# Sixteen units of the third FFN as seven block products instead of eight, in a two-layer attention/mLSTM network

## The chip, the cores and the metric

The kernel runs on one core of one Trainium2 chip. The time is device microseconds of that core, from the runs; beside it stands one profiled execution, whose span and instructions the quoted views show. In those views PE is the matrix engine (PEld its weight loads), DVE the vector engine, ACT the scalar engine, POOL is GpSimd, SP the engine that issues most transfers.

## What is computed

The reference is a network of two layers on 256 latent and 256 context tokens of width 1024. Each layer is a half FFN, a mixer (attention in the first layer, mLSTM in the second) and another half FFN, each with a modulation by `c` ahead of it and a residual with layer norm behind it. The third FFN, the first of layer 1, is the place of the change:

```
def half_ffn(h, shift, scale, gate, w_in, w_out, g, b):
    xm = modulate(h, shift, scale)
    a, u = jnp.split(xm @ w_in, 2, axis=-1)
    y = (jax.nn.silu(a) * u) @ w_out
    return post_norm(h, 0.5 * gate * y, g, b)
```

`w_in` is 1024 × 5632 (`a` and `u` have 2816 columns each), `w_out` 2816 × 1024, all in 32-bit floats.

## The kernel before

Activations lie transposed: 128 features on the partitions, 512 tokens along the row, first the latent ones (`LAT`, 256) and then the context ones (`CTX`, 256), in eight blocks of features (`ND`). Precision is kept by splitting every operand into a high part, rounded to the matrix engine's 32-bit format, and a low part, what is left. `mm3` (line 208) multiplies with three products: high × high (L211), high × low (L214), low × high (L215). `split` (line 193) makes the parts: ACT casts the high one (L194), DVE subtracts for the low one (L199).

Weights come in chunks of 128 × 1024, 512 KB. `raw` (line 173) loads one into one of `RAW` = 3 buffers by a transfer that SP issues (L179); `pair` gives one of `WB` = 7 buffers for a high and a low part; `chunk` does load and split. `Stream` splits a chunk when it is first asked for, `Keep` also holds the chunks for a second use.

`ffn` (line 525) works in 22 units of 128 hidden columns. `unit_in` makes one: for each of eight feature blocks k and the two parts `a` and `u` three products, 48 in all, of 512 columns, into two of the six PSUM buffers `mm`. `ffn_g` (line 500) then applies SiLU on ACT (L521), multiplies on DVE (L522) and splits the result. The units go in two parts of 11. After each part `unit_out` makes the outputs of eight blocks d, 33 products each, and DVE adds them with the gate to the residual `h` (L557); in the last part `add_sum` (L357) also begins the sum for the norm.

Two places work on half the columns. The first four units (`LEAD`) take `LAT` and then `CTX`, so that they can begin before the context tokens' norm is done. The last four blocks of the last part (`TAIL`) take all `LAT` outputs and then all `CTX` outputs, so that the next norm can begin. `TAILSTEP` says after which product which step of that norm is woven in: `b` begins it, `m` and `c` subtract the mean block by block, `v` makes the variance, `r` the scale, `x` the normalised blocks. `ENDSTEP` does the first steps for `CTX` behind the tail.

The modulation of later stages is made beside the FFN: `ada` (line 296) loads 512 KB of `ada_w` (L284, two buffers) and makes a dot product on DVE (L290). `pop` in `side` (line 1283) takes two from a queue after each unit and each output block of the first part; for the third FFN the queue has 32 of one dot each.

What decides the order: the instructions are traced in program order, and the framework orders each engine's queue ahead of time, earlier-traced ones first, but moves one forward whose inputs and buffers it expects ready. So chunks are loaded and split ahead of their use. An instruction that passes through `pin` (line 359) stays behind the one traced before it on its engine; the dots, the norm's products and its scale are pinned. On the chip every engine works through its queue in that fixed order.

Of the kernel before, what the change touches and what calls it, by code (L numbers as in the profile page):

```python
# [37 lines left out]
HEADS = 8  # L38
MH = 4
QK_SCALE = 128.0 ** -0.5  # L40
BIG = 1.0e30

RAW = 3
WB = 7
# [97 lines left out]
class Body:  # L142
# [137 lines left out]
    def ada_load(self, layer, dt):  # L280
        if (layer, dt // ND) not in self.mod:
            self.mod[layer, dt // ND] = self.t([P, 2, ND])
        r = self.t([P, 1024], tag="ada", bufs=2, pool=self.gp)
        self.nc.sync.dma_start(r, self.a["ada_w"][layer, dt])  # L284
        return r
# [239 lines left out]
    def ffn(self, layer, s, gate, groups, side, start=None):  # L525
        nc, V = self.nc, self.nc.vector
        li = layer * 2 + s
        allg = BOTH
        call = lambda *k: side.get(k, lambda: None)()
        with self.tc.tile_pool(name=f"ffn{li}", bufs=1) as gp:  # L530
            self.gp, self.gt, self.gw, self.gn = gp, {}, T, NFH
            done = 0
# [12 lines left out]

            def unit_out(hf, d, w, g, steps={}):
                t0, t1 = g
                y = self.mm()
                for i in range(NFH):
                    gh, gl = self.gt[hf * NFH + i]  # L550
                    self.mm3(y[:, : t1 - t0], w(d * NFH + i), (gh[:, t0:t1], gl[:, t0:t1]), i == 0, i == NFH - 1)
                    self.steps(steps.get((int(g == CTX), d - (ND - TAIL), i), ""))
                for gg in groups:
                    if gg[0] >= t0 and gg[1] <= t1:
                        v = 0 if gg[0] == 0 else 1
                        z = self.h[:, d, gg[0] : gg[1]]
                        V.scalar_tensor_tensor(z, y[:, gg[0] - t0 : gg[1] - t0], gate()[:, v, d : d + 1], z, ALU.mult, ALU.add)  # L557
                        if hf:
# [4 lines left out]
            for hf in range(2):  # L563
                js = list(range(hf * NFH, (hf + 1) * NFH))[0 if hf else done :]
# [17 lines left out]
                if not hf:  # L582
                    self.residual(len(self.later))
                w = Stream(self, [w_out[hf * NFH + i] for i in range(NFH)])
                body = ND - TAIL if hf else ND
                for d in range(body):
                    unit_out(hf, d, w, allg)
                    call("out", hf, d)
                if body < ND:
                    w = Keep(self, w.chunks, SH, w)  # L590
                    self.fine = True
                    for g in groups:
                        for d in range(body, ND):
                            unit_out(hf, d, w, g, TAILSTEP)
                    self.steps(ENDSTEP)


    def ffn_last(self, layer, gate):
# [663 lines left out]
def emit(ctx, tc, a, out):  # L1262
# [19 lines left out]

    def side(key, coef, keep=(True, True), nxt=True, ada=(), alone=False):
        def pop():
            for _ in range(3 if len(ada) > 40 else 2):
                if ada:
# [4 lines left out]
        b.begin = lambda g: b.norm(g, get, keep[0 if g == LAT else 1], nxt, alone)  # L1291
        s = {}
        for j in range(NF):
            s["in", j] = pop
# [12 lines left out]
    assert not queue[1]  # L1307
    b.ffn(1, 0, once("g2", lambda: b.half_gate(1, 2)), both, side("n3", lambda: b.ln_mod(1, 0, (1, 3)), (True, False), ada=queue[2]))
    assert not queue[2]
# [8 lines left out]
def _layout(inputs):  # L1318
# [9 lines left out]
    w = f("ffn_w_in").reshape(4, ND, P, 2, NF, P).transpose(0, 4, 2, 1, 3, 5)  # L1328
    w_in = w.reshape(4, NF, P, 2, 1024).transpose(0, 1, 3, 2, 4).reshape(4, 2 * NF, P, 1024).copy()
    A["ffn_in"] = w_in  # L1330
    A["start_in"] = w[0, :NSTART].transpose(2, 1, 0, 3, 4).reshape(ND, P, 1024)
    w = f("ffn_w_out").reshape(4, 2, NFH, P, ND, P).transpose(0, 1, 4, 2, 3, 5)
    A["ffn_out"] = w.reshape(4, 2 * NFH, 8, P, P).transpose(0, 1, 3, 2, 4).reshape(4, 2 * NFH, P, 1024)
    A["ffn_last"] = f("ffn_w_out")[1, 1].reshape(NF, P, D)
# [64 lines left out]
```

## Time and profile before

| what | us |
|---|---|
| median of 3 runs | 1701.09 |
| lowest and highest run | 1696.46 and 1701.3 |
| span of the profiled execution | 1693.6 |
| PE busy in it | 1643.8 |
| DVE busy | 1231.7 |
| ACT busy | 656.3 |

The span is the time from the first to the last instruction of one execution, so it lies a little under the times of the runs. Busy time is the time in which an engine had at least one instruction at work; engines work beside each other, so the rows don't add up. An engine's share of the whole span says little about one stage. The prediction therefore takes windows of the trace that hold one kind of work.

### The profile page before, as it was taken

The numbers are of one execution on the slowest core, as the hardware profiler recorded it, in microseconds if no ns is written. First come the engines' busy times: TensorE is split into PE (matmuls) and PEld (weight loads), VectorE is DVE, ScalarE is ACT, GpSimd is POOL, SyncE is SP. The second block draws the span as 40 slices with busy tenths as digits, with TensorE's granted clock in tenths as the row PEclk, the third lists the DMA queues.
The fourth block names the chain that finished last, engine by engine and source line by source line (L and its number), as shares of the span: only waits on it lengthen the run. The fifth ranks groups of instructions, "written<-read, shape, count | busy, mean of one in ns | idle before, by whom it ended". The sixth has DMA issues, their size and how long they took to land.

```text
span 1693.6 us, 24765 instructions
## 1 busy us (share of the span) xinstructions
PE 1643.8 (97%) x9432; PEld 1441.6 (85%) x9432; DVE 1231.7 (73%) x2681; ACT 656.3 (39%) x1125; POOL 93.6 (6%) x114
## 2 busy tenths in 40 slices
PE   7999999999899999999999999999999999999997
PEld 6888888899887898888888998888889878999986
DVE  6799977659988899996334977643335967998687
ACT  5622133215465452212331543213322645556541
POOL 0000000002321100000000100000001001120000
PEclk9999999999999999999999999999999999999999
DMA  9576765412102346774222257642221232337542
GB/s 356 184 230 231 236 210 199 149 62 77 61 2 82 119 136 234 229 244 152 93 94 75 101 179 247 215 144 98 99 100 63 94 125 76 113 125 246 178 168 94
DMA packets 71910, 250.49 MB, mean 148 GB/s; under 512 B 7920, under 2 KB 10480, under 8 KB 71792
## 3 DMA queue, kind: packets, MB, share of 16 engines
q1 hardware_dynamic: 71072, 248.15, 43.1%
q8 instruction: 74, 1.21, 0.3%
q10 hardware_dynamic: 720, 0.76, 0.1%
q14 instruction: 44, 0.36, 0.1%
HBM read 247.83 MB, written 1.05 MB: 147 GB/s over the span
## 4 chain that ended last, share of the span: by engine, by line
PE 83%; DVE 11%; ACT 3%; DMA 2%; issue 1%; POOL 0%; ACTq 0%; DVEq 0%; SPq 0%
PE t L214 23%; PE t L215 23%; PE t L211 23%; PE t L668 4%; DVE t L199 3%; PE t L1165 2%; PE t L726 2%; PE t L728 2%; PE t L727 2%; ACT t L194 1%; PE t L380 1%; DVE t L473 1%; DVE t L400 1%; DVE t L475 1%; DVE t L1201 1%
## 5 line engine op out<-in xcount | busy, mean ns | idle before, releaser
L211 PE MATMUL t<-t,t 128*128 128x512 f32 (+2 forms) x2540 | 856.1, 339 | 10.1 <-ACT t L194 7.5
L214 PE MATMUL t<-t,t 128*128 128x512 f32 (+2 forms) x2540 | 858.5, 339 | 1.8 <-DVE t L475 1.3
L215 PE MATMUL t<-t,t 128*128 128x512 f32 (+2 forms) x2540 | 854.4, 337 | 1.9 <-DVE t L199 1.9
L199 DVE TENSOR_TENSOR t<-t,t 128x256 fp32r<-128x256 f32 (+2 forms) x793 | 494.8, 659 | 196.4 <-ACT t L194 195.8
L194 ACT CAST t<-t 128x1024 fp32r<-128x1024 f32 (+2 forms) x463 | 397.7, 880 | 587.0 <-PE t L215 311.2
L211 PEld LDWEIGHTS t<-t,t 128*128 128x128 f32 x2540 | 476.6, 188 | 65.7 <-ACT t L194 9.8
L214 PEld LDWEIGHTS t<-t,t 128*128 128x128 f32 x2540 | 477.7, 188 | 56.5 <-DVE t L475 2.5
L215 PEld LDWEIGHTS t<-t,t 128*128 128x128 f32 x2540 | 477.5, 188 | 55.3 <-DVE t L199 2.8
L290 DVE SCALAR_TENSOR_TENSOR t<-t,t 128x1024 bf16<-128x1024 f32 x224 | 262.6, 1220 | 15.9 <-DMA t<-in_ada_w 15.4
L522 DVE TENSOR_TENSOR t<-t,t 128x512 f32<-128x512 f32 (+1 forms) x93 | 54.0, 585 | 112.1 <-PE t L215 92.4
L521 ACT ACTIVATE t<-t 128x512 f32<-128x512 f32 (+1 forms) x93 | 47.4, 515 | 196.9 <-PE t L215 195.0
L417 POOL TENSOR_TENSOR t<-t,t 128x256 f32<-128x256 f32 x30 | 23.3, 777 | 1161.4 <-ACT t L407 1159.9
L557 DVE SCALAR_TENSOR_TENSOR t<-t,t,t 128x256 f32<-128x256 f32 x96 | 42.7, 478 | 54.2 <-PE t L215 54.2
L726 PE MATMUL t<-t,t 128*128 128x256 f32 (+1 forms) x256 | 80.4, 316 | 0.0
L728 PE MATMUL t<-t,t 128*128 128x256 f32 (+1 forms) x256 | 79.7, 314 | 0.0
L727 PE MATMUL t<-t,t 128*128 128x256 f32 (+1 forms) x256 | 79.5, 313 | 0.0
L1165 PE MATMUL t<-t,t 128*128 128x512 f32 (+1 forms) x248 | 54.8, 373 | 11.0 <-ACT t L274 5.2
L1165 PEld LDWEIGHTS t<-t,t 128*128 128x128 f32 x248 | 46.4, 220 | 19.0 <-ACT t L274 5.2
L668 PE MATMUL t<-t,t 128*128 128x512 f32 x264 | 60.0, 389 | 0.0
L668 PEld LDWEIGHTS t<-t,t 128*128 128x128 f32 x264 | 49.5, 188 | 10.2
L407 ACT ACTIVATE t<-t 128x256 f32<-128x256 f32 x72 | 26.1, 413 | 68.3 <-DVE t L400 68.3
L726 PEld LDWEIGHTS t<-t,t 128*128 128x128 f32 x256 | 49.6, 194 | 3.1 <-DVE t L789 0.3
(164 smaller groups left out, 1067.6 us busy)
## 6 DMA issues: line engine op xcount, KB each, us to landing
t<-in_ffn_in SPq DMA_DIRECT2D x168, 512.0 KB, 4.0
t<-in_ada_w SPq DMA_DIRECT2D x139, 512.0 KB, 4.2
t<-in_ffn_out SPq DMA_DIRECT2D x66, 512.0 KB, 3.7
t<-in_ffn_last SPq DMA_DIRECT2D x22, 512.0 KB, 3.7
t<-in_att_in SPq DMA_DIRECT2D x12, 512.0 KB, 3.5
t<-in_att_out SPq DMA_DIRECT2D x8, 512.0 KB, 3.9
t<-in_ml_qk SPq DMA_DIRECT2D x8, 512.0 KB, 3.4
t<-in_ml_v SPq DMA_DIRECT2D x8, 512.0 KB, 4.0
```

Of the source, the lines that this page charges most:

```text
L194: self.behind(self.nc.scalar.copy(h, x))
L199: self.behind(self.nc.vector.tensor_tensor(out=ls, in0=xs, in1=hs.bitcast(F32), op=ALU.subtract))
L211: ins = mm(out, wh, xh, start=first, stop=False)
L214: mm(out, wh, xl, start=False, stop=False)
L215: mm(out, wl, xh, start=False, stop=last)
L290: ins = nc.vector.scalar_tensor_tensor(self.tmp().bitcast(BF16), r, 1.0, self.cb[:, v, :], ALU.mult, ALU.mult, accum_out=to)
L522: V.tensor_tensor(out=sl, in0=sl, in1=pu[:, :n], op=ALU.mult)
L668: pin(nc.tensor.matmul(ys[tt][i], gs[g], ws[k][w][:, i * 512 : (i + 1) * 512], start=k == 0 and g == w == 0, stop=k == NF - 1 and g == 1,))
L726: mm(o, self.xh[:, k, c], wh, start=k == 0, stop=False)
L727: mm(o, self.xh[:, k, c], wl, start=False, stop=False)
L728: mm(o, self.xl[:, k, c], wh, start=False, stop=k == ND - 1)
L1165: mm = lambda *k, **kw: pin(nc.tensor.matmul(*k, **kw))
```

## The change

In the third FFN the units are divided into parts of 6, 8 and 8 (`FOLD`). The first six are made as before. The other sixteen use a scheme of Strassen's kind (Winograd's form). The product of a unit is seen as a 2 × 2 block product: the weights' rows `a` and `u` against two halves of the 1024 features, and the features' halves against `LAT` and `CTX`. Eight block products become seven, each over four feature blocks and 256 columns with three products a block: 84 of 256 columns instead of 48 of 512.

- `fold_x` makes the four sums of the activations, in two calls during the outputs of the first part. Three go to new tiles, one takes the place of the `CTX` columns that nobody reads any more.
- `fold_w` makes, per unit, four sums of the weights in place in the two raw buffers, and splits the unit's first chunk, half of the second, and both buffers of sums. For the second buffer of sums DVE doesn't subtract: ACT writes the high part and its negative, and a transfer issued by GpSimd adds the raw sums to the negative.
- `folded` makes the seven products into three PSUM buffers, adding some products onto earlier ones, with copies by ACT and sums by DVE between. Two units are interleaved: the last two products of one unit stand among those of the next, and the last unit's among the first outputs.
- The layout of the weights in memory is rearranged to suit.
- The tail has six blocks (`FOLDTAIL`) with a step table of its own. `RAW` is 4 in the whole kernel, the modulation's loads have one buffer in this FFN instead of two, and the queue is emptied by `FOLDPOP`: 12 dots by the first part's units, 4, 8 and 8 by the outputs of the three parts, of which the last six are traced behind the tail. `RING` sets the space for descriptors of GpSimd's transfers to 1024 bytes.

```diff
+FOLD = {2: (6, 8, 8)}
+FOLDTAIL = 6
+FOLDPOP = ((2, 2, 2, 2, 2, 2), (4, 8, 8))
+RING = 1024
-RAW = 3
+RAW = 4
+FOLDSTEP = {(0, 5, 1): 'bmccccccc', (1, 0, 2): 'c', (1, 0, 6): 'v', (1, 2, 1): 'rxxxxxxxx'}
...
-        r = self.t([P, 1024], tag="ada", bufs=2, pool=self.gp)
+        r = self.t([P, 1024], tag="ada", bufs=self.nada, pool=self.gp)
...
+                folded = None
+                if fold and hf:
+                    folded = self.folded(js, w_in)
+                    js = []
...
-                w = Stream(self, [w_out[hf * NFH + i] for i in range(NFH)])
-                body = ND - TAIL if hf else ND
-                for d in range(body):
+                w = (Keep if fold else Stream)(self, [w_out[ends[hf] - parts[hf] + i] for i in range(parts[hf])])
+                body = ND - tail if last else ND
+                begun = 0
+                if folded:
+                    n, begun = parts[hf], 2
+                    ys = [self.mm() for _ in range(2)]
+                    part_out(hf, 0, w, allg, ys[0], range(4))
+                    next(folded)
+                    part_out(hf, 0, w, allg, ys[0], range(4, n - 1))
+                    next(folded, None)
+                    part_out(hf, 1, w, allg, ys[1], range(n - 1))
+                    for d in range(2):
+                        part_out(hf, d, w, allg, ys[d], (n - 1,))
+                        sum_out(hf, d, allg, ys[d])
+                        call("out", hf, d)
+                for d in range(begun, body):
                     unit_out(hf, d, w, allg)
                     call("out", hf, d)
+                    if fold and not hf and d in (1, 4):
+                        self.fold_x(d // 2)
...
-                            unit_out(hf, d, w, g, TAILSTEP)
+                            unit_out(hf, d, w, g, tailstep)
+                    for d in range(body, ND):
+                        call("out", hf, d)
                     self.steps(ENDSTEP)
...
+    def fold_x(self, k):
+        V, S = self.nc.vector, self.nc.scalar
+        if k == 0:
+            self.th, self.tl = (self.t([P, 3, ND // 2, TL], F32R, pool=self.gp) for _ in range(2))
+        def whole(d, g):
+            f = self.tmp().rearrange("p (d f) -> p d f", d=2)
+            h, l = (x[:, d : d + 2, g[0] : g[1]].bitcast(F32) for x in (self.xh, self.xl))
+            V.tensor_tensor(out=f, in0=h, in1=l, op=ALU.add)
+            return f
+        f11, f12, f21, f22 = whole(k, LAT), whole(k, CTX), whole(ND // 2 + k, LAT), whole(ND // 2 + k, CTX)
+        V.tensor_tensor(out=f11, in0=f11, in1=f12, op=ALU.subtract)
+        V.tensor_tensor(out=f12, in0=f22, in1=f12, op=ALU.subtract)
+        V.tensor_tensor(out=f22, in0=f22, in1=f11, op=ALU.add)
+        V.tensor_tensor(out=f21, in0=f22, in1=f21, op=ALU.subtract)
+        ks = slice(k, k + 2)
+        to = [[x[:, i, ks, :] for x in (self.th, self.tl)] for i in range(3)]
+        to3 = [x[:, ks, CTX[0] : CTX[1]] for x in (self.xh, self.xl)]
+        self.split(f11, *to[0])
+        h, l = to[1]
+        S.activation(h, f22, AF.Copy, scale=-1.0)
+        V.scalar_tensor_tensor(l, f22, -1.0, h.bitcast(F32), ALU.mult, ALU.subtract)
+        self.split(f12, *to3)
+        self.split(f21, *to[2])
...
+    def fold_w(self, j, w_in):
+        V = self.nc.vector
+        r0, r1 = (self.raw(w_in[2 * j + i]) for i in range(2))
+        a = slice(0, 512), slice(512, 1024)
+        ps = [self.pair(sh=SH)]
+        self.split(r0, *ps[0])
...
+        w22 = [x[:, c] for x in p]
+        self.split(r1[:, a[0]], *w22)
+        V.tensor_tensor(out=r1[:, a[0]], in0=r1[:, a[0]], in1=r1[:, a[1]], op=ALU.add)
+        V.tensor_tensor(out=r1[:, a[1]], in0=r1[:, a[1]], in1=r0[:, a[0]], op=ALU.add)
+        V.tensor_tensor(out=r0[:, a[0]], in0=r0[:, a[0]], in1=r1[:, a[0]], op=ALU.add)
+        V.tensor_tensor(out=r0[:, a[1]], in0=r0[:, a[1]], in1=r0[:, a[0]], op=ALU.add)
+        for r in (r0, r1):
+            p = self.pair(sh=SH)
+            if r is r1:
+                self.nc.scalar.copy(p[0], r)
+                self.nc.scalar.activation(p[1], r, AF.Copy, scale=-1.0)
+                self.nc.gpsimd.dma_start(p[1], r, accum_op=ALU.add)
+            else:
+                self.split(r, *p)
+            ps.append(p)
...
+        def begin(j):
+            w = self.fold_w(j, w_in)
+            o0, o1, o2 = (self.mm()[:, :TL] for _ in range(3))
+            sl, u = self.tmp(), self.tmp()
+            product(o0, w["11"], "b11", True)
+            S.copy(sl[:, lat], o0)
+            product(o2, w["12"], "b21", True)
+            yield
+            V.tensor_tensor(out=sl[:, lat], in0=o2, in1=sl[:, lat], op=ALU.add)
+            S.activation(sl[:, lat], sl[:, lat], AF.Silu)
+            product(o0, w["s2"], "t2", False)
+            S.copy(u[:, lat], o0)
+            product(o1, w["s3"], "t3", True)
+            yield
+            product(o0, w["s1"], "t1", False)
+            S.copy(u[:, ctx], o0)
+            V.tensor_tensor(out=u[:, ctx], in0=o1, in1=u[:, ctx], op=ALU.add)
+            yield
+            product(o0, w["s4"], "b22", False)
+            S.activation(sl[:, ctx], o0, AF.Silu)
+            yield
+            product(o1, w["22"], "t4", False)
+            V.tensor_tensor(out=u[:, lat], in0=o1, in1=u[:, lat], op=ALU.add)
...
+            V.scalar_tensor_tensor(sl, u, -1.0, sl, ALU.mult, ALU.mult)
+            self.split(sl, gh, gl)
+        before = iter(())
+        for j in js:
+            now = begin(j)
+            next(now)
+            next(before, None)
+            next(now)
+            next(before, None)
+            next(now)
+            before = now
+        return before
```

More of the change, by code (lines that the diff above doesn't have):

```diff
@@ L562, in ffn @@
             stream = lambda j: Stream(self, [w_in[2 * j + i] for i in range(2)])
-            for hf in range(2):
-                js = list(range(hf * NFH, (hf + 1) * NFH))[0 if hf else done :]
+            for hf in range(len(parts)):
+                last = hf == len(parts) - 1
+                js = list(range(ends[hf] - parts[hf], ends[hf]))[0 if hf else done :]
                 if hf == 0 and not start:
@@ L1281, in once, with side, pop @@
         return get
-    def side(key, coef, keep=(True, True), nxt=True, ada=(), alone=False):
-        def pop():
-            for _ in range(3 if len(ada) > 40 else 2):
+    def side(key, coef, keep=(True, True), nxt=True, ada=(), alone=False, fold=False):
+        def pop(n=None):
+            for _ in range(n if n is not None else 3 if len(ada) > 40 else 2):
                 if ada:
@@ L1292, in side @@
         s = {}
+        if fold:
+            for j, n in enumerate(FOLDPOP[0]):
+                s["in", j] = lambda n=n: pop(n)
+            for hf, n in enumerate(FOLDPOP[1]):
+                for d in range(ND):
+                    s["out", hf, d] = lambda n=n, d=d: pop((d + 1) * n // ND - d * n // ND)
+            return s
         for j in range(NF):
@@ L1307, in emit @@
     assert not queue[1]
[L1308 removed]
+    b.ffn(1, 0, once("g2", lambda: b.half_gate(1, 2)), both, side("n3", lambda: b.ln_mod(1, 0, (1, 3)), (True, False), ada=queue[2], fold=True))
     assert not queue[2]
```

69 lines of the change are left out of this document (61 added, 8 removed).

## Prediction

> **What bounds the kernel now.** I read the page's busy shares first, then its stages in the windows view, then the grouped instructions of the third FFN.
>
> ```profile
> span 1693.6 us, 24765 instructions
> PE 1643.8 (97%) x9432; PEld 1441.6 (85%) x9432; DVE 1231.7 (73%) x2681; ACT 656.3 (39%) x1125; POOL 93.6 (6%) x114
> ```
>
> Over the whole kernel PE is the bound. The share is an average, so I looked at the third FFN alone: its full-width products run from 998 to 1283 us, its tail of half-width ones behind that. The columns below are the window, its length, and busy microseconds with instructions of PE, PEld, DVE, ACT and POOL, then the clock and the DMA.
>
> ```profile
> 998.00:1283.00 285.00, 285.00 (x1259) 235.98 (x1258) 138.37 (x211) 76.60 (x92) 0.00 (x0) 1.00 0.45 154
> 1286.00:1296.00 10.00, 10.00 (x87) 10.00 (x86) 2.36 (x6) 0.00 (x0) 0.00 (x0) 1.00 0.03 12
> 1600.00:1620.00 20.00, 20.00 (x179) 20.00 (x178) 15.47 (x19) 10.90 (x15) 0.00 (x0) 1.00 0.47 159
> ```
>
> The first row is the changed stage: 512-column products back to back, PE busy all 285 us at full clock, DVE 138 of 285, ACT 77. Nothing waits. Whatever PE work goes there goes from the span, until another engine takes over. Counting for the two instructions that stick out over a window's edges, a 512-column product takes 285/1257 = 0.2267 us. The other two rows are stretches of 256-column products without a gap: 10/85 = 0.1176 us in one and 20/177 = 0.1130 us in the other. Half the columns thus cost half the time, plus 0 to 4%; the rows show two paces and not what chooses between them. I take the middle, 0.1153.
>
> **PE.** Sixteen units of 48 wide products (768 × 0.2267 = 174.1 us) become sixteen of 7 × 4 × 3 = 84 narrow ones (1344 × 0.1153 = 155.0; 151.9 to 158.1 at the two paces). That is **−19.1 us** (−16.0 to −22.2). The output products keep their number with parts of 6, 8 and 8. The tail now has six column blocks where it had four, so 48 wide products become 96 narrow ones: +0.2 us (0 to +0.4). A folded unit lasts 84 × 0.1153 = 9.7 us on PE.
>
> **DVE and ACT of a folded unit.** Durations by shape in the stage, mean ns of one behind the bar:
>
> ```profile
> L199 DVE TENSOR_TENSOR t<-t,t 128x1024 fp32r<-128x1024 f32 x47 | 57.5, 1224 | 65.5 <-ACT t L194 65.4
> L522 DVE TENSOR_TENSOR t<-t,t 128x512 f32<-128x512 f32 x18 | 12.4, 687 | 45.1 <-PE t L215 34.8 <-ACT t L521 10.3
> L522 DVE TENSOR_TENSOR t<-t,t 128x256 f32<-128x256 f32 x1 | 0.4, 421 | 0.3 <-ACT t L521 0.3
> L557 DVE SCALAR_TENSOR_TENSOR t<-t,t,t 128x256 f32<-128x256 f32 x22 | 9.6, 479 | 16.9 <-PE t L215 16.9
> L290 DVE SCALAR_TENSOR_TENSOR t<-t,t 128x1024 bf16<-128x1024 f32 x32 | 38.3, 1221 | 7.4 <-DMA t<-in_ada_w 7.3
> L290 DVE DVE_READ_ACCUMULATOR t<-t,t 128x1 f32 x32 | 2.6, 82 | 0.0
> ...
> L194 ACT CAST t<-t 128x1024 fp32r<-128x1024 f32 x53 | 55.8, 1053 | 139.8 <-PE t L215 95.8 <-issue 42.6
> L194 ACT CAST t<-t 128x512 fp32r<-128x512 f32 x18 | 11.1, 616 | 10.5 <-DVE t L522 10.5
> L521 ACT ACTIVATE t<-t 128x256 f32<-128x256 f32 x1 | 0.4, 385 | 1.4 <-PE t L215 1.4
> ```
>
> Back to back these overlap a little, as an entry of the timeline and one of the chain of waits show: four 256-column ones in 1.40 us, two dots with their reads in 2.30.
>
> ```profile
> 1322.45 1.40 DVE L400 TENSOR_TENSOR t<-t,t 128x256 f32<-128x256 f32 x4
> ```
>
> ```profile
> 18.68 2.30 DVE t L1201 x4
> ```
>
> So in a packed stretch a 1024-column DVE instruction costs 1.15, a 256-column one 0.35, a 512-column one by the straight line between them 0.62, an output's addition 0.41 (its 0.479 less the same 0.07).
>
> Preparing a unit's weights (`fold_w`): two wide low parts, one half-wide and four half-wide sums, 2 × 1.15 + 5 × 0.62 = 5.4. After the products: three narrow sums, one product and one low part of 512 columns, 3 × 0.35 + 2 × 0.62 = 2.3. DVE: **7.7 of 9.7 us** packed, 8.5 at full durations (2 × 1.224 + 5 × 0.687 + 3 × 0.421 + 2 × 0.687). ACT: four wide casts or negations, two half-wide casts, three narrow copies and two SiLUs, all five at 0.39: 4 × 1.05 + 2 × 0.62 + 5 × 0.39 = 7.4 of 9.7. Both fit below PE, where before DVE was half idle. Without ScalarE and the transfer, DVE would carry 8.8. For waits in this tighter weave I put **+1** us (0 to one wide DVE instruction per unit, 16 × 1.15 = 18).
>
> **The stretch before the first folded unit.** From 998 us PE has two plain units and eight outputs of 18 products: 96 × 0.2267 + 144 × 0.2267 = 54.4 us. DVE has in it: the two units 4 × 1.15 + 4 × 0.62 = 7.1; six output chunks 6.9; sixteen additions 6.6; `fold_x`, twice 12 half-wide instructions, 24 × 0.62 = 14.9; the first `fold_w` 5.4. That is 40.9. Beside it come the modulation dots, sixteen due by then. They now pass through one buffer instead of two:
>
> ```profile
> t<-in_ada_w SPq DMA_DIRECT2D x139, 512.0 KB, 4.2
> ...
> t<-in_ffn_in SPq DMA_DIRECT2D x168, 512.0 KB, 4.0
> ```
>
> ```profile
> L284 SPq DMA_DIRECT2D t<-in_ada_w x32: 327/328/427, 949.9 to 1107.4; - x32
> ```
>
> The page's rows give the time to landing, the last row the issue on SP, 0.33. One dot needs a 4.2 us landing, the issue and its own 1.3 (1.221 + 0.082): 5.8 us a turn, so 9 in 54.4 us, 9 × 1.15 = 10.4. DVE's sum is 51.3 of 54.4 us, 59 if all sixteen came. This has almost no room, and `fold_w` is a chain (cast, low part, sums, cast, low part) on which PE's third product waits: **+2** us (0 to +6). The seven dots left over add 8 us to the first 78 us of folded units, 7.7 × 8 + 8 = 70: they fit. The third pass of additions (6.6 us) lies under 192 × 0.2267 = 43.5 us of output products and costs nothing; uncovered it would be those 6.6.
>
> **The adding transfer.** No row shows a transfer that GpSimd issues, or one that adds. It can gain no more than the 1.15 us DVE step per unit that it replaces, which is counted above. The plain 512 KB land in 4.0 us, and three such (two read, one written) make 12; I take 6, nearer to the plain row. Its cover: PE's order is two products of unit j+1, one of unit j, two, one, one. The pair for the late sums comes free 36 products into a turn (4.2 us) and is first read 51 products into the next (9.7 + 5.9), 11.4 us later, of which two ACT instructions take 2.1. So 9.3 us are free: cost 0 at 6. Behind it on GpSimd nothing is queued (POOL 0.00 in the stage's row). It holds its raw buffer until it lands, and SP issues in order, so later weights stand behind that; with four buffers they have a whole turn of 9.7 us for a 4.0 us load. [...]
>
> **The end of the FFN.** Six of the last eight dots are traced behind the tail, pinned behind its last DVE addition. There DVE is full and PE already loses time:
>
> ```profile
> 1313.00:1318.00 5.00, 5.00 (x47) 5.00 (x46) 5.00 (x13) 3.36 (x7) 0.20 (x1) 1.00 0.00 0
> 1318.00:1323.00 5.00, 3.90 (x32) 3.65 (x32) 5.00 (x16) 0.90 (x4) 0.00 (x0) 1.00 0.19 56
> 1323.00:1328.00 5.00, 5.00 (x44) 4.97 (x43) 5.00 (x13) 4.31 (x11) 2.30 (x3) 1.00 0.28 105
> 1328.00:1333.00 5.00, 4.59 (x40) 4.42 (x39) 5.00 (x22) 2.51 (x5) 0.00 (x0) 1.00 0.35 116
> ```
>
> Behind a waiting dot stand the CTX norm and the next stage's low parts, and PE's pinned norm products wait for those. Six dots are 6 × 1.15 = 6.9 us of DVE; 0 to 6.9 of it reaches PE, I take half: **+3.5**. The new step table also starts the norm 6 × 3 products before the end of the tail's first half, where it was 9 × 3, so its chain has 9 × 0.1153 = 1 us less cover: **+1** (0 to 1).
>
> **A fourth raw buffer** holds for the whole kernel. It helps where PE waits for a load that waited for a buffer, as here:
>
> ```profile
> 544.00:548.00 4.00, 2.92 (x21) 2.47 (x20) 3.08 (x9) 2.33 (x3) 0.00 (x0) 1.00 0.65 200
> ```
>
> 1.08 us are lost; I take **−1** (0 to −2). The smaller descriptor scratch only gives room.
>
> **Sum.** −19.1 + 0.2 + 1 + 2 + 0 + 3.5 + 1 − 1 = −12.4 us. The profiled execution spans 1693.6 us, 7.5 under the median 1701.09 of the runs shown, so it would span 1681.2 and the median would be 1688.7, say **1689**.
>
> **Rivals.** *DVE becomes the bound.* Its durations don't overlap in this weave: 8.5 and 1.3 per 5.8 us of dots (2.2 a turn) make 10.7 against 9.7, +8 over the first eight units, and +5 before them (59 − 54.4). In place of 3 that is 13: 1688.7 + 10 = 1698.7. For it: all sixteen dots don't fit. Against: the packed rows. Chance 0.13.
>
> *The adding transfer comes late* (the slower side). Place: the third product of the pair with the late sums, once per unit. From 9.3 us on, a wait in one turn gives the next its time, so half the excess is paid per unit, and at 9.3 + 2 × 12.4/16 = 10.9 us the gain is gone. At 13 us (a little over three landings at 4.2) it costs 16 × 1.85 = 30: 1718.3. For it: an unmeasured path, up to 12 us by the bound. Against: two units of cover. Chance 0.09.
>
> *The dots at the end stop DVE.* If each of five waits for its landing in DVE's fixed order, 5 × 4.5 = 22.5 and the 6.9 replace 3.5: 1689 + 26 = 1715. Against: before the change the 32 dots of this FFN together waited 7.3 us. Chance 0.05.
>
> *The change doesn't save what it says.* Narrow products at 0.1225, half way to the 174.1/1344 = 0.1295 at which nothing is saved: +9.7, 1698. Against: both gapless rows. Chance 0.05.
>
> **Numbers.** The forecast keeps 0.68. A measurement of this kernel can tell about 0.3%, 5.1 us, from no change. Faster than 1696: 0.66 from the forecast, 0.04 from a milder DVE rival, 0.02 from the slower products: 0.72. Within: 0.02 of the forecast, 0.07 of the DVE rival, 0.03 of the products and 0.01 of the dots: 0.13. Slower than 1706.2: the transfer's 0.09, 0.04 of the dots, 0.02 of DVE: 0.15. The range reaches from 1680 (PE at 0.1130 and 5.5 of the 7.5 us of waits free, 1688.7 − 3.1 − 5.5) to 1702: the forecast with its unknowns at their upper ends (+3.1 PE, +4 before the first unit, +3.4 at the end, +2.8 in the weave), which takes in the DVE and product rivals at 1698 to 1699. The late transfer, the stopped dots and the worst of the DVE rival lie outside.
>
> **What would show it.** PE busy in the folded stretches with 84 products in 9.5 to 9.9 us and no idle rows before the products that read `s1` and `s3`; DVE at 75 to 90% there; a GpSimd queue whose 16 transfers land within 9 us; a small PE gap at the first folded unit and 2 to 5 us more idle PE behind the tail. PE waiting on DVE sums in every unit would make the first rival true; on the transfer's landing, the second; DVE waiting on `in_ada_w` behind the tail, the third.

## The result, and the profile after

| | us | runs |
|---|---|---|
| before | 1699.58 (1696.46 to 1701.30) | 5 |
| after | 1760.46 (1754.37 to 1762.97) | 5 |

The ratio is 1.0354 with a 95% interval of 1.0337 to 1.0372: 61 us slower, where 12 us faster was forecast. The profiled execution spans 1752.6 us against 1693.6, 59.0 us more. First the page of the changed kernel, its span and busy shares, the dots, the narrow products and GpSimd's transfers (in a group's row: busy us, mean ns of one, and behind the second bar the idle time before its instructions and what ended most of it).

```profile
span 1752.6 us, 26437 instructions
...
PE 1643.9 (94%) x10020; PEld 1468.1 (84%) x10020; DVE 1331.1 (76%) x2990; ACT 717.7 (41%) x1246; POOL 108.0 (6%) x130
...
L296 DVE SCALAR_TENSOR_TENSOR t<-t,t 128x1024 bf16<-128x1024 f32 x224 | 263.5, 1221 | 43.4 <-DMA t<-in_ada_w 42.8
...
L715 PE MATMUL t<-t,t 128*128 128x256 f32 x1344 | 167.2, 287 | 33.2 <-DMA t<-t 15.2
...
t<-t POOLq DMA_DIRECT2D x16, 512.0 KB, 6.3
```

PE's busy time is that of before to 0.1 us. So all 59 us are PE standing idle, and the saving in products is gone as well. The time between PE's matmuls in which none runs, added up from the trace, is 94.4 us, where it was 35.4. What PE waited for in the stage, from the view of its waits (us in total, times, longest):

```profile
PE t L386 <- DVE t L423: 17.2, 1, 17.2
PE t L715 <- DMA t<-t: 15.2, 6, 4.4
PE t L715 <- ACT t L200: 14.5, 1, 14.5
PE t L217 <- ACT t L200: 10.0, 1, 10.0
PE t L715 <- ACT t L732: 2.0, 2, 1.2
PE t L715 <- ACT t L736: 1.4, 3, 0.8
```

Three single waits make 41.7 us: one in the plain units (L217), one at the first folded unit (L715 on ACT), one behind the tail (L386, the norm's product). A fourth kind recurs: the adding transfer, 15.2 us in six waits. The wait in the plain units begins in DVE's timeline (start, length, what stood before it):

```profile
1025.83 1.22 DVE L296 SCALAR_TENSOR_TENSOR t<-t,t 128x1024 bf16<-128x1024 f32 x1 [1.76 <-DMA t<-in_ada_w]
1026.98 0.08 DVE L296 DVE_READ_ACCUMULATOR t<-t,t 128x1 f32 x1
1030.63 1.23 DVE L296 SCALAR_TENSOR_TENSOR t<-t,t 128x1024 bf16<-128x1024 f32 x1 [3.56 <-DMA t<-in_ada_w]
1031.78 0.08 DVE L296 DVE_READ_ACCUMULATOR t<-t,t 128x1 f32 x1
1035.32 1.23 DVE L296 SCALAR_TENSOR_TENSOR t<-t,t 128x1024 bf16<-128x1024 f32 x1 [3.46 <-DMA t<-in_ada_w]
1036.47 0.08 DVE L296 DVE_READ_ACCUMULATOR t<-t,t 128x1 f32 x1
1036.47 0.68 DVE L528 TENSOR_TENSOR t<-t,t 128x512 f32<-128x512 f32 x1
```

The dots come one every 4.7 us, each behind the landing of its own load, and between these three DVE does nothing. Right behind the last of a burst stands the product of a plain unit (L528); its result is cast by ACT for the outputs, and PE waits for that. The wait is paid twice, as the clock shows (columns as before: window, length, PE, PEld, DVE, ACT, POOL, granted clock, DMA).

```profile
1000.00:1040.00 40.00, 29.96 (x128) 24.42 (x127) 18.82 (x43) 6.94 (x9) 0.00 (x0) 0.91 0.54 172
...
1073.90:1087.00 13.10, 2.79 (x13) 2.79 (x14) 11.21 (x22) 6.97 (x10) 0.61 (x1) 0.50 0.32 89
...
1097.00:1174.00 77.00, 70.19 (x588) 69.20 (x587) 57.41 (x128) 45.70 (x75) 5.18 (x6) 0.97 0.58 156
...
1376.00:1396.00 20.00, 2.09 (x10) 1.82 (x10) 13.80 (x39) 8.95 (x21) 2.17 (x3) 0.63 0.65 229
```

DVE is busy for only 18.8 of 40 us in the first row, though PE waits for it. (The third row is most of the first folded part.) The work it did not do there (`fold_x`, the first weights) it does later, with hardly a pause, and it is late at the first folded unit:

```profile
1056.00:1084.00 28.00, 13.74 (x73) 11.66 (x71) 27.58 (x49) 6.56 (x11) 0.00 (x0) 0.82 0.29 87
```

ACT's timeline names the chain: a cast that waits 13.74 us for DVE's sums of `fold_x` (L652).

```profile
1065.06 0.62 ACT L200 CAST t<-t 128x512 fp32r<-128x512 f32 x1 [13.74 <-DVE t L652]
```

SP's queue stands too: from 1022.3 to 1081.9 us it issues twelve loads for dots and none of weights. No run tells what that alone costs.

Behind the tail the sum that the norm's product needs (L423) stands in DVE's order right behind the last of six dots. They come through the one buffer every 4.9 to 6.8 us, from 1361.24 to 1389.85 us. DVE stands 5.8 us in all for their landings; in the rest of the time it does other work that its order has between them.

```profile
1389.85 1.22 DVE L296 SCALAR_TENSOR_TENSOR t<-t,t 128x1024 bf16<-128x1024 f32 x1 [4.13 <-DMA t<-in_ada_w]
1391.00 0.08 DVE L296 DVE_READ_ACCUMULATOR t<-t,t 128x1 f32 x1
1391.00 0.42 DVE L423 TENSOR_TENSOR t<-t,t 128x256 f32<-128x256 f32 x1
```

### The profile page after: what moved, and what is told of

Same layout as the page of the kernel before. It is cut to its first block, busy times and chain, and to the rows that moved or that the text cites. A ratio compares the mean times of both kernels' runs of the same rounds, so it can differ in the third digit from the quotient of the medians.

```text
span 1752.6 us, 26437 instructions
## 1 busy us (share of the span) xinstructions
PE 1643.9 (94%) x10020; PEld 1468.1 (84%) x10020; DVE 1331.1 (76%) x2990; ACT 717.7 (41%) x1246; POOL 108.0 (6%) x130
## 4 chain that ended last, share of the span: by engine, by line
PE 70%; DVE 14%; DMA 8%; issue 4%; ACT 3%; POOL 0%; SPq 0%; ACTq 0%; DVEq 0%; POOLq 0%
PE t L217 18%; PE t L221 18%; PE t L220 18%; PE t L715 4%; DVE t L205 4%; PE t L829 3%; DMA t<-in_ada_w 3%; DMA t<-t 3%; PE t L1326 2%; ACT t L200 1%; PE t L889 1%; PE t L887 1%; PE t L888 1%; PE t L386 1%; DVE t L296 1%
## 5 line engine op out<-in xcount | busy, mean ns | idle before, releaser
L217 PE MATMUL t<-t,t 128*128 128x512 f32 (+2 forms) x2288 | 759.6, 334 | 21.0 <-ACT t L200 16.9
L220 PE MATMUL t<-t,t 128*128 128x256 f32 (+2 forms) x2288 | 761.7, 334 | 1.7 <-DVE t L481 1.3
L221 PE MATMUL t<-t,t 128*128 128x256 f32 (+2 forms) x2288 | 758.1, 333 | 2.4 <-DVE t L205 2.4
L200 ACT CAST t<-t 128x1024 fp32r<-128x1024 f32 (+2 forms) x485 | 411.7, 868 | 581.5 <-PE t L221 243.9
L205 DVE TENSOR_TENSOR t<-t,t 128x256 fp32r<-128x256 f32 (+2 forms) x956 | 518.8, 584 | 154.2 <-ACT t L200 153.6
L217 PEld LDWEIGHTS t<-t,t 128*128 128x128 f32 x2288 | 431.1, 189 | 67.0 <-ACT t L200 19.8
L220 PEld LDWEIGHTS t<-t,t 128*128 128x128 f32 x2288 | 433.3, 190 | 46.3 <-DVE t L481 2.4
L221 PEld LDWEIGHTS t<-t,t 128*128 128x128 f32 x2288 | 432.6, 189 | 46.2 <-DVE t L205 3.3
L296 DVE SCALAR_TENSOR_TENSOR t<-t,t 128x1024 bf16<-128x1024 f32 x224 | 263.5, 1221 | 43.4 <-DMA t<-in_ada_w 42.8
L715 PE MATMUL t<-t,t 128*128 128x256 f32 x1344 | 167.2, 287 | 33.2 <-DMA t<-t 15.2
L715 PEld LDWEIGHTS t<-t,t 128*128 128x128 f32 x1344 | 164.3, 197 | 36.4 <-DMA t<-t 16.5
L528 DVE TENSOR_TENSOR t<-t,t 128x512 f32<-128x512 f32 (+1 forms) x77 | 43.0, 564 | 70.5 <-PE t L221 60.4
L527 ACT ACTIVATE t<-t 128x512 f32<-128x512 f32 (+1 forms) x77 | 37.9, 498 | 142.0 <-PE t L221 140.9
L576 DVE SCALAR_TENSOR_TENSOR t<-t,t,t 128x256 f32<-128x256 f32 x112 | 49.8, 479 | 40.1 <-PE t L221 39.9
L423 POOL TENSOR_TENSOR t<-t,t 128x256 f32<-128x256 f32 x30 | 23.2, 773 | 892.6 <-ACT t L413 891.1
L1326 PEld LDWEIGHTS t<-t,t 128*128 128x128 f32 x248 | 46.7, 222 | 19.4 <-ACT t L280 5.0
L829 PEld LDWEIGHTS t<-t,t 128*128 128x128 f32 x264 | 49.5, 188 | 10.2
```

The lines of the kernel that those rows point to most:

```text
L200: self.behind(self.nc.scalar.copy(h, x))
L205: self.behind(self.nc.vector.tensor_tensor(out=ls, in0=xs, in1=hs.bitcast(F32), op=ALU.subtract))
L217: ins = mm(out, wh, xh, start=first, stop=False)
L220: mm(out, wh, xl, start=False, stop=False)
L221: mm(out, wl, xh, start=False, stop=last)
L296: ins = nc.vector.scalar_tensor_tensor(self.tmp().bitcast(BF16), r, 1.0, self.cb[:, v, :], ALU.mult, ALU.mult, accum_out=to)
```

## The experiments

Theory A: the loss is that of the 32 dots. They pass through one buffer and are pinned in DVE's order, so DVE stands for each landing with everything behind it; the adding transfer is a smaller, separate price. The rival B: the folded units themselves, with their transfer, sums and casts, are too tight, and the dots only lie beside that. Each ratio is to runs of the kernel before on the same chip, with a 95% interval. The kernel before took 1696.8 to 1699.6 us in these groups of runs, so a difference of two times from different sections is sure to 2 or 3 us only.

### Two buffers for the dots

```diff
-RING = 1024
+RING = 512
-            self.nada = 1 if fold else 2
+            self.nada = 2
```

> The changed kernel with two buffers for the modulation's loads instead of one (the descriptor space halved to make room). Theory A: the 32 dots, drawn through one buffer, make DVE stand in its fixed order before each dot until its load has landed; that is most of the loss. A expects the DVE waits on in_ada_w in the third FFN (36 us in the changed kernel) to fall below 15 us, the PE gap of 10 us in the fifth unit to go, and a time of 1700 to 1722 us. Theory B: the folded weave itself (sums on DVE, adding transfers) is what PE waits for. B expects 1745 us or more, with the gap of 14 us at the first folded unit still there.

Measured: 1726.8 us, ratio 1.0167 (1.0151 to 1.0182). One buffer costs 33.7 of the 61 us, 5 us less than A's range asked for. DVE's waits for the loads fall from 36.4 to 9.8 us. Behind the tail the six dots now start within 13.8 us instead of 28.6, and the wait there falls from 17.2 to 2.9 us at most, that of the plain units from 10.0 to 3.9, that at the first folded unit from 14.5 to 3.5. PE's waits for the transfer stay (15.4 us in seven).

### No dots

```diff
-                    b.ada(*ada.pop(0))
+                    x = ada.pop(0)
+                    if x[0] == 0 or x[1] < 40:
+                        b.ada(*x)
...
+    for ch in range(5, 9):
+        b.mod[1, ch] = b.t([P, 2, ND])
+        V.memset(b.mod[1, ch], 0.1)
```

> The changed kernel with the third FFN's 32 modulation loads and dots left out (constants stand in their place). Theory A: without them the gaps before the first folded unit and behind the tail go, and what stays is the PE saving of 19 us less some 1 to 1.5 us of waits per folded unit: 1695 to 1706 us. Theory B: the first folded unit still comes 10 us or more late and the time stays above 1730 us.

Measured: 1703.1 us, ratio 1.0031 (1.0020 to 1.0041). The dots cost 57.4 us in this kernel, and without them it is still 0.3% slower than before. So A holds for most of the loss, but there is a second price, at least as large as what the change saves. (This kernel leaves out the dots' loads as well. That their traffic is not the main price is shown by the run with two buffers, which has the same loads.) PE's waits that are left in the folded parts:

```profile
PE t L715 <- DMA t<-t: 8.8, 4, 2.3
PE t L715 <- ACT t L732: 5.0, 5, 1.9
PE t L715 <- ACT t L736: 3.0, 4, 0.8
```

### No dots, the third low part by DVE

```diff
-            if r is r1:
+            if False:
```

> As the one without dots, and the third wide low part is made by DVE like the other two, without the negative copy and the adding transfer. If the transfer's lateness is what PE waits for in the folded units (4 to 5 us in eight units of the changed kernel), it is 4 to 12 us faster than the one without dots; if DVE at 8.8 of 9.7 us is the limit, it is 3 to 15 us slower.

Measured: 1679.5 us, ratio 0.9896 (0.9880 to 0.9913). Without the transfer the kernel is 23.6 us faster, though DVE has more to do. That was twice what I had expected at most. The groups of PE in the folded parts, first of the kernel without dots (its first part), then of this one (both parts):

```profile
L715 PE MATMUL t<-t,t 128*128 128x256 f32 x648 | 79.5, 285 | 9.4 <-DMA t<-t 4.2 <-ACT t L732 3.6 <-ACT t L736 1.6
```

```profile
L715 PE MATMUL t<-t,t 128*128 128x256 f32 x1344 | 159.7, 281 | 0.0
```

In the second row no product waits. So 159.7 us for 1344 is what the narrow products cost in this run without any wait.

### The kernel before with one buffer

```diff
-        r = self.t([P, 1024], tag="ada", bufs=2, pool=self.gp)
+        r = self.t([P, 1024], tag="ada", bufs=self.nada, pool=self.gp)
...
+            self.nada = 1 if li == 2 else 2
```

> The kernel before with one alone of the changes: one buffer instead of two for the modulation's loads in the third FFN. Theory A: DVE stands before eight dots in a row behind the lead units here too, and the fifth unit's product waits: 8 to 30 us slower than before (1708 to 1730). Theory B: DVE has room for the waits in this kernel, within 5 us of before.

Measured: 1712.95 us, ratio 1.0087 (1.0072 to 1.0102). One buffer alone, in a kernel without any folded unit, costs 15 us. Its waits, of DVE and of PE, from 990 to 1110 us:

```profile
DVE t L290 <- DMA t<-in_ada_w: 20.2, 17, 3.9
```

```profile
PE t L211 <- DVE t L522: 7.7, 1, 7.7
```

The same 32 dots had waited 7.3 us with two buffers. DVE's product of a plain unit again stands behind them. This speaks against B for that part of the loss.

### The changed kernel with the third low part by DVE

The edit is that of the run without dots: `if r is r1` becomes `if False`.

> The changed kernel with the third wide low part made by DVE (no negative copy, no adding transfer), dots in one buffer as in the changed kernel. Theory A (the adding transfer costs PE waits of its own, beside the dots): 10 to 28 us faster than the changed kernel, 1732 to 1750 us. Rival (the transfer's waits lie in the shadow of the dots' waits, and DVE has more to do): within 6 us of the changed kernel, 1754 or more.

Measured: 1734.99 us, ratio 1.0221 (1.0207 to 1.0235). The three long waits are there as before (10.1, 14.4 and 18.0 us), and those for the transfer are gone with it. It gains 25.5 us beside the dots and 23.6 without them: two causes that hardly depend on each other.

### Two buffers, and the third low part by DVE

> Both: two buffers for the modulation's loads and the third wide low part by DVE. If the two losses add up (34 us by the second buffer, 24 by the transfer), 1760 - 58 = 1702, some 1696 to 1710 us. If the dots in the folded weave load DVE to its limit, 1715 or more, since DVE gets 1.15 us more per unit.

Measured: 1697.4 us in 10 runs, ratio 0.9999 (0.9990 to 1.0008). Both cures together bring the kernel back to the time before and no further. The dots with two buffers still cost 1697.4 − 1679.5 = 17.9 us, and PE's gaps are 46.4 us against 31.0: eight of the 32 still stand in a burst behind the lead units, where PE waits 2.9 and then 3.5 us, and six behind the tail.

### A fifth raw buffer

What makes the transfer cost? It lands in 6.3 us, as I had assumed, and yet PE waits. Theory T1: it holds one of four raw buffers until it lands, SP's queue stands for that buffer (112.3 us in sixteen waits, below), and so the next unit's weights come late. T2: the chain within one unit is too long. GpSimd's timeline in the kernel without dots:

```profile
1105.71 0.86 POOL L690 DMA_DIRECT2D t<-t  x1 [8.77 <-ACT t L689]
1119.83 0.85 POOL L690 DMA_DIRECT2D t<-t  x1 [13.26 <-PE t L715]
1129.52 0.88 POOL L690 DMA_DIRECT2D t<-t  x1 [8.83 <-ACT t L689]
```

Two units take 23.8 us from issue to issue (1105.71 to 1129.52), where two turns of 84 products take 2 × 84 × 159.7/1344 = 20.0. In SP's waits of the same kernel the raw loads stand for the transfer sixteen times:

```profile
SPq L185 <- DMA t<-t: 112.3, 16, 9.4
```

```diff
-RAW = 4
+RAW = 5
```

> The changed kernel without the third FFN's dots (left out, constants in their place), with a fifth raw weight buffer. Theory T1: PE's waits for the adding transfer come from the raw buffer that each transfer holds until it lands: the next load waits for the landing, then the sums, the casts and the next transfer follow. A fifth buffer opens that loop: PE's waits in the folded units fall from some 17 to under 6 us, and the time from 1703 to 1690 or less. Theory T2: the loop runs through the seven buffers of split weights or ACT's fixed order, or the landing itself is too long: 1698 or more.

Measured: 1697.9 us in 10 runs, ratio 1.0004 (0.9994 to 1.0015). Five of the 23.6 us, 0.1 us below what T2 expected at least. T1 missed here: PE's waits in the folded parts are 14.0 us against 16.8, those for the transfer even 11.1 against 8.8. SP still stands for the transfer, 110.9 us in sixteen waits, so one more buffer did not open the loop.

### Eight pairs for the split weights

```diff
-RING = 1024
+RING = 512
-WB = 7
+WB = 8
-        return self.t([P, 16], tag="small", bufs=18)[:, :w]
+        return self.t([P, 16], tag="small", bufs=17)[:, :w]
```

> The changed kernel without the 32 dots, with the adding transfer, and with eight buffers for the split weights instead of seven. If what makes the transfer cost is that it holds back the next pair of buffers (with a fifth raw buffer ScalarE's casts waited for PE's reads of a pair), the waits of PE for it go and the time is at or below 1690 us. If the loop runs through the raw buffer and the transfer's own landing, the pairs do not matter: 1699 to 1705 us.

Measured: 1706.1 us, ratio 1.0045 (1.0031 to 1.0060). The time is no shorter, but PE's waits in the folded parts show that this does not settle it:

```profile
PE t L715 <- ACT t L732: 12.1, 8, 2.6
...
PE t L715 <- DMA t<-t: 1.1, 1, 1.1
```

The waits for the transfer are nearly gone, as the first theory said; those for ACT's copies rise from 8.0 to 12.1 us. In all, PE's gaps fall from 48.6 to 44.2 us, but its busy time rises from 1640.0 to 1650.2. The smaller descriptor space and one small buffer fewer make the room for the pairs, and products are slower far from the third FFN too: from 600 to 900 us, 294 of 1163 full-width ones take 232 to 234 ns from start to start, where 1 of 1192 does in the kernel without dots (nearly all take 226 or 227). (The profiled execution is also the slowest of the six, 1710.8 us.) So the run has a price of its own, and whether pairs have a share in the 23.6 us stays open.

### Buffers of their own for the sums that the transfer reads

```diff
-RAW = 4
+RAW = 3
...
-        V.tensor_tensor(out=r1[:, a[0]], in0=r1[:, a[0]], in1=r1[:, a[1]], op=ALU.add)
-        V.tensor_tensor(out=r1[:, a[1]], in0=r1[:, a[1]], in1=r0[:, a[0]], op=ALU.add)
+        rs = self.t([P, 1024], tag="rs2", bufs=2, pool=self.gp)
+        V.tensor_tensor(out=rs[:, a[0]], in0=r1[:, a[0]], in1=r1[:, a[1]], op=ALU.add)
+        V.tensor_tensor(out=rs[:, a[1]], in0=r1[:, a[1]], in1=r0[:, a[0]], op=ALU.add)
+        r1 = rs
```

> The changed kernel without the 32 dots and with the adding transfer, but the second sums of weights are written to two buffers of their own, and the transfer reads from there: three raw buffers, which come free as soon as DVE has made its sums, however long the transfer takes. Theory T1 (the price of the transfer is that it holds a raw buffer until it lands, so that the next unit's load, its casts and, in ScalarE's fixed order, the copies that PE needs come late): SP's waits for the transfer go, and the time falls from 1703 to 1680 to 1688 us. T2 (the chain of one unit, load, sums, cast, negation, transfer, is by itself too long for the turn): 1697 us or more, with PE's waits for the transfer still there.

Measured: 1690.6 us, ratio 0.9959 (0.9946 to 0.9973). As many buffers as with five raw ones, but now no load waits for a transfer: SP's waits on it are gone, and 12.5 of the 23.6 us with them. That is T1's mechanism, at half the price; the time lies between the two ranges. PE's waits in the folded parts:

```profile
PE t L717 <- DMA t<-t: 4.7, 7, 1.1
PE t L717 <- ACT t L734: 2.6, 2, 1.4
```

They are about a half and a third of what they were (8.8 for the transfer, 8.0 for ACT's copies). The other 11 us stay open: the waits on the transfer that are left speak for T2, and ACT, which makes the cast and the negation in one order with the copies that PE waits for (2.6 us in two waits), may have a share, as may the pairs. No run took these apart.

### All dots in the second FFN

The third low part is DVE's; the 32 dots go behind the 40 of the second FFN, where pops are then of three while more than 36 are left.

> A version that may beat both: the third wide low part by DVE, and the 32 dots moved into the second FFN (two buffers, three at a time, then two), where DVE has room beside 285 us of products. All of the reference is computed. If the second FFN hides them: as the kernel without dots and with DVE low parts, 1679 to 1685 us, 0.99 of before. If they disturb the second FFN as they did the third, 1690 or more, with PE gaps there.

Measured: 1698.2 us in 11 runs, ratio 1.0005 (0.9993 to 1.0016). The folded parts are nearly free of waits, but the loss has moved with the dots. The profiled execution is the fastest of the eleven, 1692.7 us, so it shows no more than 13 of the 18.7 us by which this kernel is slower than the one without dots. PE's longest wait of the second FFN in it, and DVE's:

```profile
PE t L217 <- DVE t L528: 6.5, 2, 6.0
```

```profile
DVE t L296 <- DMA t<-in_ada_w: 10.4, 17, 1.2
```

Here the dots have two buffers and wait little each. But the pops of four units, twelve loads with two dots each where there were eight loads, are traced in one burst behind the four lead units, and the product of the fifth unit stands behind them all. This suggests that what a dot costs is a matter of its place: a burst ahead of an instruction that PE waits for. The next run tests it.

### The dots spread

```diff
-FOLDPOP = ((2, 2, 2, 2, 2, 2), (4, 8, 8))
+FOLDPOP = ((0, 0, 0, 0, 2, 2), (0, 8, 0))
...
-        [(1, p, both2) for p in range(40)],
-        [(1, p, (0,)) for p in range(40, 72)],
+        [(1, p, both2) for p in range(40)] + [(1, p, (0,)) for p in range(40, 60)],
+        [(1, p, (0,)) for p in range(60, 72)],
```

With the third low part by DVE; pops in the second FFN stay at two.

> The third low part is DVE's; all 32 dots are computed, 20 of them in the second FFN behind its own 40, still two a unit, and 12 in the third: two behind each of the units 4 and 5, one behind each output block of the middle part; none behind the four lead units in a burst, none behind the tail. Theory A (a dot costs where several stand one behind the other in DVE's fixed order behind one buffer, and elsewhere only its own 1.3 us of a DVE that has room): 1680 to 1687 us, near the 1679.5 us without the dots, and no PE gap over 3 us in the third FFN. Rival B (every dot costs about 0.6 us wherever it stands, as the 18.7 us for 32 dots in the run with all of them in the second FFN would say): 1695 to 1702 us.

Measured: 1684.4 us, ratio 0.9922 (0.9910 to 0.9934). All seven products, all dots, one buffer in the third FFN, and faster than both kernels; A's range. PE's longest gap in the third FFN is 2.4 us.

### The same, with wide low parts

```diff
                 if fold and hf:
+                    self.fine = False
                     folded = self.folded(js, w_in)
```

`split` cuts a wide low part into four of 256 columns while `fine` is set, and `fine` is cleared only behind the seventh plain unit. The folded FFN has six, so the flag stays set throughout, which I had not seen: four of 256 take 1.43 us (as in DVE's timeline of the changed kernel), one of 1024 takes 1.15 packed.

> The kernel with the spread dots, and in the folded parts each wide low part as one DVE instruction of 1024 columns instead of four of 256. If DVE is near the bound there, the shorter work (about 0.2 us for each of three low parts of a unit) gives 2 to 5 us; if the folded parts had no waits left, as the run without dots and transfer showed, it gives 0 to 1 us.

Measured: **1679.56 us**, ratio 0.9892 (0.9879 to 0.9905), 4.9 us faster than with the narrow ones, as expected of a DVE near its bound. PE's waits in the folded parts fall from 3.4 to 0.9 us, but most of the gain is in PE's busy time, 1633.6 to 1629.9: with fewer waits less of it lies in stretches of half clock (18.4 us, then 14.8; see the end), which explains half of that. Its page and its waits of PE in the folded parts:

```profile
span 1677.6 us, 26246 instructions
...
PE 1629.9 (97%) x10020; PEld 1456.8 (87%) x10020; DVE 1334.8 (80%) x2880; ACT 701.4 (42%) x1230; POOL 93.8 (6%) x114
...
L296 DVE SCALAR_TENSOR_TENSOR t<-t,t 128x1024 bf16<-128x1024 f32 x224 | 262.7, 1220 | 13.0 <-DMA t<-in_ada_w 12.4
```

```profile
PE t L716 <- ACT t L733: 0.9, 2, 0.6
```

The dots are as many and as long as in the changed kernel (224, 1220 ns), and DVE is busier; but it stands 13.0 us for them and not 43.4. PE is idle for 33.5 us between matmuls, about as long as before the change, and busy for 14 us less.

## Why the prediction was wrong

**The step that failed first: the dots through one buffer.** The stretch before the first folded unit, +2 (0 to +6), counted how many dots one buffer lets through (9 of 16, at 5.8 us a turn; measured, they came every 4.7) and charged 1.15 us of DVE's time for each, "the seven dots left over" being made later. That takes for granted that other work of DVE goes on while a dot waits for its landing. At the plain units it did not: a dot is pinned in DVE's order, and DVE stood before it, busy for 18.8 of 40 us. The price is the landing, with all that is queued behind: 10.0 us at the plain units and 14.5 at the first folded one instead of 2. What stands behind a waiting dot had been asked in the text for the end of the FFN only.

**The dots at the end: +3.5 (0 to +6.9), and 17.2 came.** Here the prediction had the mechanism as a rival, at 1715 us and a chance of 0.05. It argued against it with the 7.3 us that the 32 dots had waited before. But that row was of two buffers, and a second buffer is just what hid the landings: with it DVE's waits for the loads of the changed kernel fell from 36.4 to 9.8 us. With one, the kernel before itself lost 15 us. The rival let DVE stand for five landings, 22.5 us; it stood 5.8 us and worked in between, and yet the norm's sum came only behind the sixth dot. As a whole the rival was too small, since it saw the end and not the start: all three places, with what follows from them, make 57.4 us.

**The second step that failed: the adding transfer, put at 0.** Its duration was right: 6.3 us against the 6 taken, with 9.3 of cover. What failed is the sentence behind that: "with four buffers they have a whole turn of 9.7 us for a 4.0 us load". The transfer holds its raw buffer from the load through sums, cast, negation and landing, and SP's queue stands behind it sixteen times (112.3 us in the kernel without dots). Cover for the transfer's reader was counted, cover for its source was not. The price of the transfer is 23.6 us. Buffers of their own for its source took 12.5 of them away, so that much is shown to be the source's; the rest stays open. The rival of a late transfer (1718) had the place and nearly the size, for the wrong reason: it needed 13 us a landing.

**PE: −19.1 (−16.0 to −22.2)**: the products alone saved less. 159.7 and 156.9 us for the 1344 (the two runs without long waits) against 174.1 give −14.4, outside the range, and −17.2, inside it. Both paces were there again: from start to start 1321 of 1334 products took about 118 ns in the run without any wait, 515 of 1328 in the last run, and in the changed kernel, with its many waits, most (952 of 1222 at full clock) about 113. So the pace is not a constant of the product; what chooses it stays open. The change without its two mistakes gives 1679.5 − 1698.1 = −18.6 us in the run without dots, and −19.2 with them (1679.56 − 1698.73), there with the wide low parts too. That this is so near to −19.1 is in part luck: other waits fell as well (PE's gaps are 31.0 us in the run without dots, 35.4 before).

**The weave: +1** (0 measured where dots and transfer are away). **DVE's share** came near: 8.8 of 9.7 us, or 91%, without the transfer, and 69.09 of 77 us, 90%, in that run's first folded part. Some luck is in it, since each wide low part had been counted at 1.15 us and the kernel made it as four in 1.43. The row:

```profile
1054.00:1131.00 77.00, 77.00 (x651) 76.73 (x650) 69.09 (x166) 43.21 (x74) 0.00 (x0) 1.00 0.39 121
```

At 90% it carried PE without a gap. So the transfer that was to relieve DVE took away a step that was hidden.

**FOLDSTEP +1 and the raw buffer −1**: behind the tail the run without dots and transfer has PE gaps of 0.61, 0.53 and 2.23 us, the kernel before 1.10, 0.41, 2.02 and 1.24. No loss to the new step table is seen. PE's gaps ahead of 960 us and behind 1420 us add up to 29.3 us in the kernel before and to 27.1 in that run. But they vary from 26.4 to 28.7 us among the other runs with four raw buffers (without the one that disturbs the second FFN), and the run with three has 27.8: the raw buffer's share is not shown.

**What came on top: the clock.** The prediction took every wait at its length. In the changed kernel PE's busy time is 14.0 us longer than in the best version with the same products, because behind the three long waits the granted clock was 0.50 and the products slow (to 1043.1, 1087.5 and 1401.5 us, where the waits end at 1037.9, 1084.2 and 1393.4; the first is shown below): 46.7 us of its busy time lie in stretches of half clock, against 14.8 in that version, and half of the difference is 16 us.

## What to carry to other kernels

Before a buffer is taken away, look at who stands behind the instruction that waits for it: in a fixed order the price can be the whole landing, times the instructions in a burst (here a dot every 4.7 us, and PE waits of 10.0, 14.5 and 17.2 us), and a small wait in the old profile (7.3 us here) may be small because of that very buffer. A transfer that replaces an engine's step has two ends: ask when its reader needs it, and also which buffer it holds until it lands, and which queue stands behind that buffer (12.5 of the transfer's 23.6 us went with buffers of its own). Side work was cheap when it was spread one or two at a time over stretches where its engine has room (1684.4 us with all dots), and dear as a burst ahead of something that the bound engine needs (1698.2 us).

## What the runs showed of the hardware

In the changed kernel PE's granted clock was 0.50 for a while behind some of its waits and stayed at 1.00 behind others. PE's 10.0 us wait runs from 1027.8 to 1037.8 us; the windows around its end, and then those of two shorter waits, 3.08 us from 1133.6 on and 2.15 us from 1156.5 on:

```profile
1033.00:1038.00 5.00, 0.14 (x1) 0.14 (x1) 2.23 (x7) 0.81 (x2) 0.00 (x0) 0.50 0.39 107
1038.00:1043.00 5.00, 5.00 (x12) 3.90 (x13) 1.77 (x3) 0.30 (x1) 0.00 (x0) 0.50 0.37 121
```

```profile
1131.90:1135.30 3.40, 1.65 (x14) 1.45 (x13) 3.07 (x7) 0.95 (x3) 0.00 (x0) 1.00 1.00 260
1135.30:1138.70 3.40, 2.07 (x18) 2.07 (x19) 1.43 (x4) 2.96 (x4) 0.08 (x1) 1.00 0.40 90
...
1155.80:1159.20 3.40, 1.25 (x11) 1.05 (x10) 2.25 (x6) 2.53 (x5) 0.00 (x0) 1.00 0.66 130
1159.20:1162.60 3.40, 3.40 (x18) 3.40 (x18) 0.67 (x2) 1.38 (x2) 0.88 (x1) 0.50 0.79 245
```

For 5 us after the first wait only 12 full-width products go through, where 22 go at full clock (5/0.2267). The granted clock goes to 0.50 at 1032.9 us, 5.1 us into that wait, and back to 1.00 at 1043.1 us. The length alone does not tell what follows a wait: behind the one of 2.15 us the clock was 0.50 from 1159.2 to 1162.6 us, behind the one of 3.08 us it stayed at 1.00. What decides between the two was not shown.

The adding transfer of 512 KB within the core's memory, issued by GpSimd, took 0.86 us to issue and landed in 6.3 us (median of sixteen; 5.2 to 7.4) beside a DVE that was busy for about three quarters of the folded parts (57.41 of 77 us from 1097 us on). The prediction's 6 was itself a guess. Why such a transfer took longer than the 4.0 us of the kernel before's plain loads of 512 KB was not shown.
